# A two-layer encoder trunk: one-hot addition of the last two expert units, earlier gate weights, an earlier embedding product and x scaled ahead of its transposition

## Chip, cores and metric

The kernel runs on one core of one Trainium2 chip. The metric is device time in microseconds, lower is better: 1538.12 us, the median of three runs (1536.56 to 1542.2).

## What is computed

Two layers over 512 tokens of width 1024, all in float32. Each layer has attention in two branches, then a mixture of 32 experts, then a gated embedding. The part around the change, cut from the reference:

```python
x = x + hierarchical_moe(rmsnorm(x, g_ffn[i]), ...)   # top-1 of 4 groups, then top-2 of 8 experts
# per expert: hid = silu(xb @ w_gate[e]) * (xb @ w_up[e]); y = hid @ w_down[e]
# out[token] += gate * y, two experts per token
ple_gate = jax.nn.sigmoid(rmsnorm(x, g_ple[i]) @ w_ple_gate[i])
x = x + (p[i] @ w_ple[i]) * ple_gate
```

## The kernel before

The rows of x (512 x 1024) lie in on-chip memory as four tiles of 128 tokens. All other large buffers are slots of 8 KB per partition in one arena, numbered 0 to 18 (and 20); in odd layers slots 0 to 3 and 15 to 18 change places (`place`). PSUM has two banks for `proj`, two for `av` and four for `z`, each handed out in turn in the order of the program. The order of the instructions on an engine is set ahead of time by a scheduler that goes by the program's order and by estimated times; `tc.issue_after` puts one instruction behind another by hand. Each engine and each queue then works in that order.

**Experts.** The 32 experts are taken in pairs, with room for 64 tokens each, so that a unit is 128 rows on both halves of the array; a 17th unit in the middle takes tokens of an expert with more. The loop over units is at L1221. A unit goes through `fetch` (POOL gathers its rows), `turn` (transpositions, L1143), `up` (32 first-stage products, L1160, then the activation, `act`) and, one iteration later, `finish`: `down` (transposition L1172, copy `hid` L1174, 16 second-stage products L1179), two copies out of PSUM and a scatter by POOL's indirect DMA into `ybuf` in HBM (L1192). Weights come in loads of 1 MB on the SP queue (L1015), as far ahead as slots are free; `expert_slots` lays down which.

**Embedding.** Six units ahead of the end the loop loads the embedding rows (`praw`, L1226) and `w_ple`; `ple_rows` transposes and splits them five units ahead of the end (L1205), and `ple_product(t)` multiplies one tile of 128 tokens (12 products, L116 to L118) in each of the next four iterations, between a `down` and the next `up`.

**float32 products in three.** `split` makes two parts of a value: ACT copies it, rounded, to `hi` (L139, L142), VectorE forms the rest, `lo` (L140, L143). `mm` does hi x hi, lo x hi and hi x lo. Each gate weight is 8 such pieces (`Stream.split`); `gcol` is the norm's gain.

**The end of the experts.** All units but the last are scattered. When they are in `ybuf`, SP loads it back, both results of each token side by side (`yg`, L1257, four loads of 1 MB), with the first loads of the gate weights (L329) between them. `stored(t)` adds both to x with the token's gates `gm2` (L1267). The last unit isn't scattered: its result is split into `y`, a matrix `which` with a one where row and token meet is built, and a product with it (L1282) brings the rows to their tokens; L1285 adds them with the gates `gl`. `after` computes `gm2` and `gl` behind the routing. Then come, for each tile, the sum of squares (L1287), the reciprocal root `r` (L1289, L1290) and `turn_in`, which transposes x, unscaled, and splits it into `gT` (L289, L139, L140).

**The gate.** Two halves of two weights each; in each, four tiles by two weights (`PAIRED`), 24 products of 256 columns apiece. For each result the sigmoid is made of Abs, Exp, Ln and Exp on ACT with `r` as the scale of Abs (L1335), and on VectorE `pz = min(p r, 0)` (L1339) and a subtraction (L1340); then come the product with the embedding (L1343) and the addition to x (L1344). The third and fourth gate weight reuse the buffers of the first two for their `hi` part, so they are split behind the first half's products. In layer 0 POOL loads the next layer's first weight meanwhile (L1298).

Of the kernel before, what the change touches and what calls it, by code (L numbers as in the profile page):

```python
# [23 lines left out]
D = 1024  # L24
# [37 lines left out]
def trunk(ctx: ExitStack, tc: tile.TileContext, a, out):  # L62
# [240 lines left out]
    def turn_in(xs, hT, t):  # L303
        for h, p in transposed(xs):
            split(p, hT.t[h][:, :, t * 128:(t + 1) * 128])

    class Stream:
# [3 lines left out]
        def __init__(self, srcs, raws, his=(7, 8), pieces=1, first=(), eng=nc.vector, pool=(), depth=None, quick=()):  # L311
# [7 lines left out]
            self.nsplit = 0  # L319

# [53 lines left out]

        def get(self, ahead=1):
# [20 lines left out]
    for l in range(L):  # L396
# [3 lines left out]
        ws2 = Stream([(a["wple"][l], (128, 2, D))] + [(a["wpg"][l, c], std, gcol[:, 1]) for c in range(4)], (10, 6, 4, 9), his=(7, 8), pieces=8, first=(5,))  # L400
# [647 lines left out]
        def after():  # L1048
# [5 lines left out]
            gl2 = keep.tile([128, 2, NT], F32, name="gl2")  # L1054
            nc.vector.tensor_tensor(gl2, fo[:, :, :, NP - 1], fo[:, :, :, NE - 1], op=OP.add)
            nc.vector.scalar_tensor_tensor(gl2, rt, float(CAP), gl2, op0=OP.is_lt, op1=OP.mult)
            nc.vector.tensor_tensor(gl2, gl2, gm2, op=OP.mult)
            nc.vector.tensor_tensor(gm2, gm2, gl2, op=OP.subtract)
            nc.vector.tensor_tensor(gl, gl2[:, 0], gl2[:, 1], op=OP.add)
# [14 lines left out]
        gl = keep.tile([128, NT], F32, name="gl")  # L1074
# [91 lines left out]
        def down(u, sg):  # L1166
# [7 lines left out]
            nc.scalar.activation(hid, pt[:, :2 * n].rearrange("p (c n) -> p c n", c=2), AF.Copy)  # L1174
# [23 lines left out]
        halves, whole = [None], [None]  # L1198
# [10 lines left out]
        def ple_product(t):  # L1209

            wp = ws2.done[0]
            if t % 2 == 0:
                pp[t // 2] = slot(11 + t // 2, [128, 2, D], F32, f"pp{t // 2}")
            for h in range(2):
                p = p_proj()
                with tc.issue_after(halves[0]):
                    whole[0] = mm(p, lambda k: pT[:, k, t * 128:(t + 1) * 128], lambda k: wp[:, k, h * 512:(h + 1) * 512], 2).ins
                nc.scalar.activation(pp[t // 2][:, t % 2, h * 512:(h + 1) * 512], p, AF.Copy)

        last = None  # L1220
        for i, u in enumerate(units):  # L1221
            if i + 2 < len(units):
                gs.append(fetch(units[i + 2]))
            if i == len(units) - 6:
# [5 lines left out]
            if i == len(units) - 5:  # L1230
                ple_rows()
            if i == len(units) - 1:
                finish(*last)
# [202 lines left out]
```

## Time and profile before

| | |
|---|---|
| median of the runs | 1538.12 us (1536.56 to 1542.2) |
| profiled execution | 1539.81 us, its span 1538.1 us |
| mean granted TensorE clock | 0.976 |
| TensorE busy | 1453.9 us (95%) |
| VectorE busy | 714.8 us (46%) |
| ACT busy | 669.5 us (44%) |
| POOL busy | 114.8 us (7%) |
| DMA | 325.42 MB, mean 212 GB/s |

Times in the profile count from the first instruction. PE is TensorE, DVE is VectorE, ACT is ScalarE, SP and POOL issue DMAs; a q behind a name is that engine's instruction queue. A timeline's line gives start, length, engine, line of the kernel, operation, output<-input with shapes and count, and in brackets the idle time before it and what ended it. Matmuls overlap, so their single lengths are longer than their distance. Granted clock 1.00 is 2.4 GHz, 0.50 is 1.2 GHz.

### The profile page before, as it was taken

The numbers are of one execution on the slowest core, as the hardware profiler recorded it, in microseconds if no ns is written. First come the engines' busy times: TensorE is split into PE (matmuls) and PEld (weight loads), VectorE is DVE, ScalarE is ACT, GpSimd is POOL, SyncE is SP. The second block draws the span as 40 slices with busy tenths as digits, with TensorE's granted clock in tenths as the row PEclk, the third lists the DMA queues.
The fourth block names the chain that finished last, engine by engine and source line by source line (L and its number), as shares of the span: only waits on it lengthen the run. The fifth ranks groups of instructions, "written<-read, shape, count | busy, mean of one in ns | idle before, by whom it ended". The sixth has DMA issues, their size and how long they took to land. (4 is left out here: it accounts for less than half of the span.)

```text
span 1538.1 us, 21263 instructions
## 1 busy us (share of the span) xinstructions
PE 1453.9 (95%) x8212; PEld 1007.8 (66%) x8212; DVE 714.8 (46%) x1606; ACT 669.5 (44%) x1448; POOL 114.8 (7%) x113
## 2 busy tenths in 40 slices
PE   8999999999989998888999999999999999979886
PEld 7767886888963333336897688778898533334386
DVE  5574675544452121218836746654535321122186
ACT  5674455543322222325836745655532222222166
POOL 0000000000111111010210000000002111110002
PEclk9999999999989999998999999999999999999998
DMA  7210224325389999985121111252363899999731
GB/s 299 96 46 13 107 83 157 112 89 219 138 302 416 418 412 414 422 343 215 71 108 55 56 55 59 81 197 83 102 274 113 350 419 420 377 418 422 315 134 55
DMA packets 60780, 325.42 MB, mean 212 GB/s; under 512 B 11429, under 2 KB 11685, under 8 KB 28033
## 3 DMA queue, kind: packets, MB, share of 16 engines
q1 hardware_dynamic: 50272, 302.10, 49.8%
q0 software_dynamic: 9248, 17.70, 3.1%
q10 hardware_dynamic: 1152, 4.19, 0.7%
q8 instruction: 67, 1.10, 0.3%
q14 instruction: 41, 0.33, 0.1%
HBM read 312.04 MB, written 28.84 MB: 222 GB/s over the span
## 5 line engine op out<-in xcount | busy, mean ns | idle before, releaser
L1160 PE MATMUL proj<-raw,gT 128*64 128x512 f32 x1056 | 261.5, 600 | 4.1 <-issue 3.0
L140 DVE TENSOR_TENSOR wlo<-raw,whi 128x1024 fp32r<-128x1024 f32 (+1 forms) x108 | 121.4, 1141 | 125.4 <-ACT whi L139 123.9
L1160 PEld LDWEIGHTS proj<-raw,gT 128*64 128x64 f32 x1056 | 81.8, 137 | 146.1 <-issue 143.5
L1179 PE MATMUL z<-raw,hid 128*64 128x512 f32 x528 | 155.6, 636 | 2.0 <-ACT hid L1174 1.9
L139 ACT ACTIVATE whi<-raw 128x1024 fp32r<-128x1024 f32 (+1 forms) x108 | 104.8, 990 | 77.1 <-PE proj L117 45.6
L811 POOL TENSOR_TENSOR xs<-x,gb 128x512 f32<-128x512 f32 (+2 forms) x34 | 45.6, 1343 | 974.1 <-DVE x L855 809.2
L147 ACT ACTIVATE sgm<-proj 128x256 f32<-128x256 f32 (+1 forms) x34 | 13.0, 384 | 208.5 <-PE proj L1160 208.5
L117 PE MATMUL proj<-wlo,gTh 128*128 128x256 f32 x336 | 98.0, 292 | 4.6 <-DVE wlo L143 4.6
L1179 PEld LDWEIGHTS z<-raw,hid 128*64 128x64 f32 x528 | 45.2, 144 | 82.5 <-issue 73.0
L116 PE MATMUL proj<-whi,gTh 128*128 128x256 f32 x336 | 97.5, 290 | 1.4 <-ACT gTh L139 1.4
L118 PE MATMUL proj<-whi,gTl 128*128 128x256 f32 x336 | 97.5, 290 | 0.0
L1147 DVE COPY gT<-av 128x512 f32<-128x512 f32 (+1 forms) x32 | 21.5, 671 | 149.7 <-PE proj L1160 113.8
L118 PE MATMUL proj<-gTh,wlo 128*128 128x512 f32 x192 | 75.6, 394 | 0.0
L118 PE MATMUL proj<-hTh,wlo 128*128 128x512 f32 x192 | 75.6, 394 | 0.0
L117 PE MATMUL proj<-hTl,whi 128*128 128x512 f32 x192 | 75.6, 394 | 0.0
L117 PE MATMUL proj<-gTl,whi 128*128 128x512 f32 x192 | 75.6, 394 | 0.0
L116 PE MATMUL proj<-hTh,whi 128*128 128x512 f32 x192 | 75.5, 393 | 0.0
L116 PE MATMUL proj<-gTh,whi 128*128 128x512 f32 x192 | 75.5, 393 | 0.0
L116 PE MATMUL proj<-whi,mh 128*128 128x256 f32 x256 | 74.0, 289 | 0.0
L117 PE MATMUL proj<-wlo,mh 128*128 128x256 f32 x256 | 72.9, 285 | 0.0
L118 PE MATMUL proj<-whi,ml 128*128 128x256 f32 x256 | 72.6, 284 | 0.0
L117 PEld LDWEIGHTS proj<-wlo,gTh 128*128 128x128 f32 x336 | 65.9, 196 | 6.1 <-DVE wlo L143 6.0
(341 smaller groups left out, 3299.2 us busy)
## 6 DMA issues: line engine op xcount, KB each, us to landing
raw<-in_wgu_dram SPq DMA_DIRECT2D x132, 1024.0 KB
raw<-in_wdn_dram SPq DMA_DIRECT2D x66, 1024.0 KB
raw<-in_win_dram SPq DMA_DIRECT2D x37, 1024.0 KB
raw<-in_wo_dram SPq DMA_DIRECT2D x8, 1024.0 KB
yg<-ybuf SPq DMA_DIRECT2D x8, 1024.0 KB
raw<-in_wpg_dram SPq DMA_DIRECT2D x8, 1024.0 KB
ybuf<-zero SPq DMA_DIRECT2D x8, 512.0 KB
brw<-in_bra_dram SPq DMA_DIRECT2D x16, 256.0 KB
```

The lines of the kernel that those rows point to most:

```text
L116: nc.tensor.matmul(o, lhs.hi, rhs.hi, start=start, stop=False, **kw)
L117: nc.tensor.matmul(o, lhs.hi, rhs.lo, start=False, stop=False, **kw)
L118: return nc.tensor.matmul(o, lhs.lo, rhs.hi, start=False, stop=stop, **kw)
L139: r = nc.scalar.activation(dst.hi, src, AF.Copy)
L140: split_lo[0] = eng.tensor_tensor(dst.lo, src, f(dst.hi), op=OP.subtract)
L147: nc.scalar.activation(dst, src, AF.Abs)
L811: nc.gpsimd.tensor_tensor(xs[t][:, cs], x[:, t][:, cs], gb[:, cs], op=OP.mult)
L1147: nc.vector.tensor_copy(gT[h], src)
L1160: nc.tensor.matmul(p[r:r + CAP], gT[h][:, k, r:r + CAP], w[:, k], start=h + k == 0, stop=h + k == 4, tile_position=(0, r), skip_group_chec ...
L1179: halves[0] = nc.tensor.matmul(py[r:r + CAP], hid[:, c, r:r + CAP], w[:, c, h * 512:(h + 1) * 512], start=c == 0, stop=c == 1, tile_positi ...
```

## The change

- `praw` and `w_ple` are loaded 8 units ahead of the end, transposed 7 ahead; the eight half-tile products are done in six iterations: two, two, one, one, one, one.
- The last two units aren't scattered: unit 15's result is split into `y0` (slot 3) ahead of the last unit, the last one's into `y1`. `which`, `gl` and the one-hot products exist twice. `yg` lies in slots 0, 1, 2, 5.
- SP issues gate weight 1 ahead of `yg` 0, then weight 2, `yg` 1, weight 3, `yg` 2, `yg` 3; weight 4 goes into `yg` 1's slot, loaded behind tile 1. Weight 1's first four pieces are split behind unit 15's split and ahead of `y1`'s; weight 3 has `hi` in slot 9 and is split behind the last tile's transposition.
- x of each tile is scaled by `r` on ACT into `yg`'s second half, and this is transposed; the gate uses `sigmoid` without a scale.

```diff
         for h, p in transposed(xs):
-            split(p, hT.t[h][:, :, t * 128:(t + 1) * 128])
+            r = split(p, hT.t[h][:, :, t * 128:(t + 1) * 128])
+        return r, split_lo[0]
     class Stream:
...
                 self.done[i] = w
+        def begin(self, i):
+            self.load(i)
+            self.nsplit += 1
+            shape = list(self.srcs[i][1])
+            self.done[i] = Pair(slot(self.his[(self.nsplit - 1) % len(self.his)], shape, F32R, "whi"), self.low[i])
+        def piece(self, i, c):
+            w, c = self.done[i], slice(c, c + 1)
+            hi = split(self.raw[i][:, c], w[:, c], self.srcs[i][2][:, c])
+            self.apart(hi, self.pieced.setdefault(i, []), split_lo[0])
+            return hi, split_lo[0]
         def get(self, ahead=1):
...
         ws1 = streams[l]
-        ws2 = Stream([(a["wple"][l], (128, 2, D))] + [(a["wpg"][l, c], std, gcol[:, 1]) for c in range(4)], (10, 6, 4, 9), his=(7, 8), pieces=8, first=(5,))
+        ws2 = Stream([(a["wple"][l], (128, 2, D))] + [(a["wpg"][l, c], std, gcol[:, 1]) for c in range(4)], (10, 6, 4, 10, 1), his=(7, 8, 7, 9, 8), pieces=8, first=(5,))
         if l == 0:
...
             nc.vector.tensor_tensor(gm2, gate, bad, op=OP.mult)
-            gl2 = keep.tile([128, 2, NT], F32, name="gl2")
-            nc.vector.tensor_tensor(gl2, fo[:, :, :, NP - 1], fo[:, :, :, NE - 1], op=OP.add)
-            nc.vector.scalar_tensor_tensor(gl2, rt, float(CAP), gl2, op0=OP.is_lt, op1=OP.mult)
-            nc.vector.tensor_tensor(gl2, gl2, gm2, op=OP.mult)
-            nc.vector.tensor_tensor(gm2, gm2, gl2, op=OP.subtract)
-            nc.vector.tensor_tensor(gl, gl2[:, 0], gl2[:, 1], op=OP.add)
+            for j in range(2):
+                u = NP - 2 + j
+                gl2 = keep.tile([128, 2, NT], F32, name="gl2")
+                nc.vector.tensor_tensor(gl2, fo[:, :, :, u], fo[:, :, :, NP + u], op=OP.add)
+                nc.vector.scalar_tensor_tensor(gl2, rt, float(CAP), gl2, op0=OP.is_lt, op1=OP.mult)
+                nc.vector.tensor_tensor(gl2, gl2, gm2, op=OP.mult)
+                nc.vector.tensor_tensor(gm2, gm2, gl2, op=OP.subtract)
+                nc.vector.tensor_tensor(gl[:, j], gl2[:, 0], gl2[:, 1], op=OP.add)
             nc.vector.scalar_tensor_tensor(sp, rt, -float(CAP - 1), sp, op0=OP.add, op1=OP.mult)
...
             ws2.get(0)
-        def ple_product(t):
+        def ple_product(t, h):
             wp = ws2.done[0]
-            if t % 2 == 0:
+            if t % 2 == 0 and not h:
                 pp[t // 2] = slot(11 + t // 2, [128, 2, D], F32, f"pp{t // 2}")
-            for h in range(2):
-                p = p_proj()
-                with tc.issue_after(halves[0]):
-                    whole[0] = mm(p, lambda k: pT[:, k, t * 128:(t + 1) * 128], lambda k: wp[:, k, h * 512:(h + 1) * 512], 2).ins
-                nc.scalar.activation(pp[t // 2][:, t % 2, h * 512:(h + 1) * 512], p, AF.Copy)
+            p = p_proj()
+            with tc.issue_after(halves[0]):
+                whole[0] = mm(p, lambda k: pT[:, k, t * 128:(t + 1) * 128], lambda k: wp[:, k, h * 512:(h + 1) * 512], 2).ins
+            nc.scalar.activation(pp[t // 2][:, t % 2, h * 512:(h + 1) * 512], p, AF.Copy)
         last = None
...
                 gs.append(fetch(units[i + 2]))
-            if i == len(units) - 6:
+            if i == len(units) - 8:
                 praw = slot(12, [128, NT, 256], F32, "praw")
...
                 ws2.load(0)
-            if i == len(units) - 5:
+            if i == len(units) - 7:
                 ple_rows()
             if i == len(units) - 1:
-                finish(*last)
                 break
...
             last, curT = (u, sg), nxtT
-            if i >= len(units) - 5:
-                ple_product(i - len(units) + 5)
-        which = wk.tile([128, 512], F32R, name="which", tag="gT", bufs=4)
+            if i >= len(units) - 7:
+                for k in ((0, 1), (2, 3), (4,), (5,), (6,), (7,))[i - len(units) + 7]:
+                    ple_product(k // 2, k % 2)
         tokens = wk.tile([128, 512], F32, name="tokens", tag="gT", bufs=4)
         nc.gpsimd.iota(tokens, pattern=[[1, 512]], base=0, channel_multiplier=0, allow_small_or_imprecise_dtypes=True)
-        token = wk.tile([128, 1], F32, name="token")
-        nc.vector.tensor_copy(token, idx[:, u:u + 1])
-        nc.vector.tensor_scalar(which, tokens, token, None, op0=OP.is_equal)
-        ygs = []
-        for t in range(NT):
-            ygs.append(slot(t, [128, 2, D], F32, "yg"))
-            nc.sync.dma_start(ygs[t], ybuf.rearrange("(i t p) d -> t p i d", i=2, p=128)[t])
-            if t < 2:
-                ws2.load(t + 1)
-        ws2.split(1)
-        sg = up(u, curT)
-        ws2.split(2)
-        def stored(t):
-            for i in range(2):
-                nc.vector.scalar_tensor_tensor(x[:, t], ygs[t][:, i], gm2[:, i, t:t + 1], x[:, t], op0=OP.mult, op1=OP.add)
-        gT = Halves([15, 16, 17, 18], "gT")
-        stored(0)
-        y = slot(20, [128, 2, D], F32R, "y")
-        for h, py in enumerate(down(u, sg)):
-            split(py, Pair(y[:, 0, h * 512:(h + 1) * 512], y[:, 1, h * 512:(h + 1) * 512]))
-        ws2.load(3)
-        ws2.load(4)
-        for t in range(NT):
-            if t:
-                stored(t)
+        which = []
+        def find(u):
+            which.append(wk.tile([128, 512], F32R, name="which", tag="gT", bufs=4))
+            token = wk.tile([128, 1], F32, name="token", tag="token", bufs=2)
+            nc.vector.tensor_copy(token, idx[:, u:u + 1])
+            nc.vector.tensor_scalar(which[-1], tokens, token, None, op0=OP.is_equal)
+        ys = [slot(3, [128, 2, D], F32R, "y0"), None]
+        def halved(j, py, h):
+            y = ys[j]
+            return split(py, Pair(y[:, 0, h * 512:(h + 1) * 512], y[:, 1, h * 512:(h + 1) * 512]))
+        def added(j, t):
             for h in range(2):
...
                 for c in range(2):
-                    nc.tensor.matmul(p, which[:, t * 128:(t + 1) * 128], y[:, c, h * 512:(h + 1) * 512],
+                    nc.tensor.matmul(p, which[j][:, t * 128:(t + 1) * 128], ys[j][:, c, h * 512:(h + 1) * 512],
                                      start=c == 0, stop=c == 1)
                 xc = x[:, t][:, h * 512:(h + 1) * 512]
-                nc.vector.scalar_tensor_tensor(xc, p, gl[:, t:t + 1], xc, op0=OP.mult, op1=OP.add)
+                nc.vector.scalar_tensor_tensor(xc, p, gl[:, j, t:t + 1], xc, op0=OP.mult, op1=OP.add)
+        find(last[0])
+        for h, py in enumerate(down(*last)):
+            halved(0, py, h)
+        before = hidden[0], split_lo[0]
+        ygs = []
+        for t in range(NT):
+            if t < 3:
+                ws2.load(t + 1)
+            ygs.append(slot((0, 1, 2, 5)[t], [128, 2, D], F32, "yg"))
+            nc.sync.dma_start(ygs[t], ybuf.rearrange("(i t p) d -> t p i d", i=2, p=128)[t])
+        sg = up(u, curT)
+        find(u)
+        def stored(t):
+            for i in range(2):
+                nc.vector.scalar_tensor_tensor(x[:, t], ygs[t][:, i], gm2[:, i, t:t + 1], x[:, t], op0=OP.mult, op1=OP.add)
+        gT = Halves([15, 16, 17, 18], "gT")
+        ws2.begin(1)
+        with tc.issue_after(before[0].ins), tc.issue_after(before[1].ins):
+            parts = [ws2.piece(1, c) for c in range(4)][-1]
+        stored(0)
+        added(0, 0)
+        stored(1)
+        added(0, 1)
+        ys[1] = slot(20, [128, 2, D], F32R, "y1")
+        for h, py in enumerate(down(u, sg)):
+            with tc.issue_after(parts[0].ins), tc.issue_after(parts[1].ins):
+                results = halved(1, py, h)
+        for c in range(4, KT):
+            ws2.piece(1, c)
+        ws2.split(2)
+        for t in range(NT):
+            if t > 1:
+                stored(t)
+                added(0, t)
+            added(1, t)
             ss = npool.tile([128, 1], F32, name="ss", tag="ss", bufs=4)
...
             nc.scalar.activation(r, r, AF.Exp, scale=-0.5)
-            turn_in(x[:, t], gT, t)
+            for h in range(2):
+                nc.scalar.activation(ygs[t][:, 1, h * 512:(h + 1) * 512], x[:, t][:, h * 512:(h + 1) * 512], AF.Copy,
+                                     scale=r)
+            last_turn = turn_in(ygs[t][:, 1], gT, t)
+            if t == 1:
+                ws2.load(4)
+        with tc.issue_after(last_turn[0].ins), tc.issue_after(last_turn[1].ins):
+            ws2.split(3)
         work2.close()
...
                 p = banks[t] if wide else banks[t][:, cc * 256:(cc + 1) * 256]
-                r = rs[:, t:t + 1]
                 with tc.high_priority() if not wide else ExitStack():
-                    s = wk.tile([128, 512], F32, name="ps", tag="ps", bufs=3)[:, :n]
-                    nc.scalar.activation(s, p, AF.Abs, scale=r)
-                    nc.scalar.activation(s, s, AF.Exp, scale=-1.0)
-                    nc.scalar.activation(s, s, AF.Ln, bias=1.0)
-                    z = wk.tile([128, 512], F32, name="pz", tag="pz", bufs=3)[:, :n]
-                    nc.vector.tensor_scalar(z, p, r, 0.0, op0=OP.mult, op1=OP.min)
-                    nc.vector.tensor_tensor(s, z, s, op=OP.subtract)
-                    nc.scalar.activation(s, s, AF.Exp)
+                    s = wk.tile([128, 512], F32, name="ps", tag="ps", bufs=4)[:, :n]
+                    sigmoid(s, p)
                     cs = slice(c0 * 256, c0 * 256 + n)
```

## Rows read from the trace of the kernel before

**Rows 1.** Timeline of TensorE at the embedding's transpositions, both layers

```profile
619.56 1.97 PE L1205 MATMUL z<-ident,praw 128*128 128x128 f32 x8 [5.09 <-DMA praw<-in_p_dram]
...
1380.18 1.97 PE L1205 MATMUL z<-ident,praw 128*128 128x128 f32 x8 [4.76 <-DMA praw<-in_p_dram]
...
1383.05 4.78 PE L1179 MATMUL z<-raw,hid 128*64 128x512 f32 x16 [0.47 <-ACT hid L1174]
```

**Rows 2.** Timeline of the SP queue, layer 1: start, us, line, what is issued

```profile
1323.20 4.45 SPq L1015 DMA_DIRECT2D raw<-in_wdn_dram  x2
...
1359.02 0.33 SPq L1226 DMA_DIRECT2D praw<-in_p_dram  x1
...
1450.61 0.38 SPq L1257 DMA_DIRECT2D yg<-ybuf  x1
```

**Rows 3.** Busy time by stretch, layer 1: us, each engine's busy us, granted clock, DMA share, GB/s

```profile
1335.00:1340.00 5.00, 5.00 (x24) 1.70 (x22) 1.01 (x2) 0.38 (x1) 1.96 (x2) 1.00 0.97 346
...
1380.00:1385.00 5.00, 4.35 (x16) 2.66 (x18) 2.73 (x5) 3.81 (x7) 0.00 (x0) 0.50 1.02 423
...
1435.00:1440.00 5.00, 5.00 (x20) 2.59 (x15) 0.69 (x1) 1.20 (x2) 0.99 (x1) 1.00 0.89 374
...
1440.00:1445.00 5.00, 5.00 (x25) 2.23 (x26) 0.69 (x1) 1.19 (x2) 0.00 (x0) 1.00 0.47 189
...
1450.00:1455.00 5.00, 1.31 (x6) 0.29 (x2) 1.27 (x3) 2.01 (x5) 0.00 (x0) 0.86 0.69 247
...
1465.00:1470.00 5.00, 2.33 (x11) 1.81 (x11) 5.00 (x11) 2.14 (x5) 0.00 (x0) 0.73 1.04 424
```

**Rows 4.** Timeline of TensorE from the last product to the gate, layer 1

```profile
1437.08 0.51 PE L116 MATMUL proj<-whi,pT 128*128 128x512 f32 x1
...
1440.08 3.70 PE L1179 MATMUL z<-raw,hid 128*64 128x512 f32 x16
...
1443.57 7.09 PE L1160 MATMUL proj<-raw,gT 128*64 128x512 f32 x32
...
1453.93 0.66 PE L1172 MATMUL z<-ident,sgm 128*128 128x128 f32 x2 [3.28 <-DVE sgm L1081]
...
1455.06 6.31 PE L1179 MATMUL z<-raw,hid 128*64 128x512 f32 x16 [0.47 <-ACT hid L1174]
...
1466.19 0.39 PE L116 MATMUL proj<-whi,gTh 128*128 128x256 f32 x1 [0.69 <-ACT gTh L139]
...
1471.29 0.41 PE L118 MATMUL proj<-whi,gTl 128*128 128x256 f32 x1
...
1482.65 1.18 PE L1282 MATMUL z<-y,which 128*128 128x512 f32 x4
```

**Rows 5.** Busy time by stretch where the second pair of gate weights is split

```profile
740.00:745.00 5.00, 2.72 (x13) 2.32 (x14) 4.97 (x10) 3.75 (x10) 2.01 (x3) 0.87 0.57 210
...
1500.00:1526.00 26.00, 24.14 (x194) 23.33 (x192) 21.24 (x38) 20.34 (x46) 5.97 (x4) 1.00 0.11 41
```

**Rows 6.** POOL's scatter of a unit's results, layer 1, and how long scatters take to land

```profile
1438.63 0.99 POOL L1192 DMA_INDIRECT ybuf<-ring,dst  x1 [11.54 <-DVE ring L1189]
...
DMA to landing us min/median/max: 8.5/8.5/8.6
```

**Rows 7.** Groups by shape between 1440 and 1500 us: count, busy us, mean ns

```profile
L1267 DVE SCALAR_TENSOR_TENSOR x<-yg,gm,x 128x1024 f32<-128x1024 f32 x8 | 10.1, 1276 | 0.0
...
L1285 DVE SCALAR_TENSOR_TENSOR x<-z,gl,x 128x512 f32<-128x512 f32 x8 | 5.8, 745 | 0.2
...
L1287 ACT ACTIVATE yg<-x 128x1024 f32<-128x1024 f32 x4 | 4.2, 1055 | 2.5 <-DVE x L1285 2.5
...
L139 ACT ACTIVATE gTh<-z 128x512 fp32r<-128x512 f32 x8 | 4.7, 594 | 8.8 <-PE z L289 8.8
...
L140 DVE TENSOR_TENSOR gTl<-z,gTh 128x512 fp32r<-128x512 f32 x8 | 5.5, 690 | 1.8 <-ACT gTh L139 1.6
...
L1339 DVE TENSOR_SCALAR pz<-proj,rs 128x512 f32<-128x512 f32 x2 | 1.5, 748 | 0.2 <-ACT ps L1335 0.2
```

More of the change, by code (lines that the diff above doesn't have):

```diff
@@ L319, in __init__ @@
             self.nsplit = 0
+            self.pieced = {}
         def load(self, i, eng=nc.sync, parts=1):
@@ L1073, in trunk @@
         gm2 = wt("gm2", [128, 2, NT])
-        gl = keep.tile([128, NT], F32, name="gl")
+        gl = keep.tile([128, 2, NT], F32, name="gl")
         routing.close()
@@ L1173, in down @@
             hid = wk.tile([128, 2, 128], F32, name="hid", tag="hid", bufs=2)[:, :, :n]
-            nc.scalar.activation(hid, pt[:, :2 * n].rearrange("p (c n) -> p c n", c=2), AF.Copy)
+            hidden[0] = nc.scalar.activation(hid, pt[:, :2 * n].rearrange("p (c n) -> p c n", c=2), AF.Copy)
             for h in range(2):
@@ L1196, in trunk @@
         pp = [None, None]
-        halves, whole = [None], [None]
+        halves, whole, hidden = [None], [None], [None]
         def ple_rows():
@@ new lines, in halved @@
+        def halved(j, py, h):
[3 more added lines that the diff above has]
+            for h in range(2):
+                p = p_z()
+                for c in range(2):
+                    nc.tensor.matmul(p, which[j][:, t * 128:(t + 1) * 128], ys[j][:, c, h * 512:(h + 1) * 512],
+                                     start=c == 0, stop=c == 1)
+                xc = x[:, t][:, h * 512:(h + 1) * 512]
+                nc.vector.scalar_tensor_tensor(xc, p, gl[:, j, t:t + 1], xc, op0=OP.mult, op1=OP.add)
@@ L1269, in trunk @@
         gT = Halves([15, 16, 17, 18], "gT")
+        ws2.begin(1)
+        with tc.issue_after(before[0].ins), tc.issue_after(before[1].ins):
+            parts = [ws2.piece(1, c) for c in range(4)][-1]
         stored(0)
-        y = slot(20, [128, 2, D], F32R, "y")
+        added(0, 0)
+        stored(1)
+        added(0, 1)
+        ys[1] = slot(20, [128, 2, D], F32R, "y1")
         for h, py in enumerate(down(u, sg)):
-            split(py, Pair(y[:, 0, h * 512:(h + 1) * 512], y[:, 1, h * 512:(h + 1) * 512]))
-        ws2.load(3)
-        ws2.load(4)
+            with tc.issue_after(parts[0].ins), tc.issue_after(parts[1].ins):
[3 more added lines that the diff above has]
+        ws2.split(2)
         for t in range(NT):
-            if t:
+            if t > 1:
                 stored(t)
-            for h in range(2):
-                p = p_z()
-                for c in range(2):
-                    nc.tensor.matmul(p, which[:, t * 128:(t + 1) * 128], y[:, c, h * 512:(h + 1) * 512],
-                                     start=c == 0, stop=c == 1)
-                xc = x[:, t][:, h * 512:(h + 1) * 512]
-                nc.vector.scalar_tensor_tensor(xc, p, gl[:, t:t + 1], xc, op0=OP.mult, op1=OP.add)
+                added(0, t)
+            added(1, t)
             ss = npool.tile([128, 1], F32, name="ss", tag="ss", bufs=4)
@@ L1290, in trunk @@
             nc.scalar.activation(r, r, AF.Exp, scale=-0.5)
-            turn_in(x[:, t], gT, t)
+            for h in range(2):
+                nc.scalar.activation(ygs[t][:, 1, h * 512:(h + 1) * 512], x[:, t][:, h * 512:(h + 1) * 512], AF.Copy,
[5 more added lines that the diff above has]
+            ws2.split(3)
         work2.close()
```

## Prediction

> **What bounds the kernel now.** I read the busy shares first, then TensorE's timeline through the last expert units, then the busy time by stretch, and last the queues that feed them (SP and POOL). TensorE is busy for 95% of the span, so time can come only from places where it waits or runs at its lower clock. The end of each layer has three. Numbers are of layer 1 unless said otherwise; layer 0 shows the same sequence some 760.6 us earlier (the same transposition at 619.56 and at 1380.18 [rows 1]).
>
> First, the embedding's rows: TensorE stands for 5.09 us (layer 0) and 4.76 us until `praw` lands [rows 1]. The reader is to see that SP issues it at 1359.02 [rows 2], 21.2 us before the first transposition, behind a full queue (share 1.02), and that the granted clock afterwards is 0.50 (1.2 GHz) [rows 3]: the 16 second-stage products of a unit take 4.78 us there [rows 1] and 3.70 at the full clock [rows 4].
>
> Second, the passage from the last unit to the gate: that unit's first stage starts at 1443.57 and takes 7.09, its activation leaves TensorE idle for 3.28, the second stage runs at the low clock (6.31), and the gate's first product at 1466.19 has its third only at 1471.29 [rows 4]. From 1465 on VectorE is busy for 5.00 of 5 us and TensorE for 2.33 [rows 3]. What ends this passage is a chain: the scatter of unit 15, `yg` issued behind it at 1450.61 [rows 2], sums on VectorE, transpositions.
>
> Third, the passage between the two pairs of gate weights: TensorE has 2.72 of 5 us in layer 0, and 24.14 of 26 in layer 1 [rows 5].
>
> **Embedding earlier.** Today TensorE wants `praw` 16.4 us after its issue and gets it after 21.2. Two units earlier the issue follows the load at 1323.20 [rows 2], where fewer bytes move (346 GB/s, later 423) [rows 3] and less is queued. I take the wait as gone, with its 4.76 us and the clock's 1.08: the last unit starts 5.8 us earlier, near 1437.8. Lower bound 0 (the wait moves along). The eight products only change place. Before unit 14's results are scattered 3.5 tiles' worth of them stand in place of 3; a tile takes 3.0 us (1437.08 to 1440.08) [rows 4]. That scatter thus starts 5.8 - 1.5 = 4.3 us before 1438.63 [rows 6], at 1434.3.
>
> At 1335 the DMA share is 0.97 at 346 GB/s [rows 3]. The Trainium skill, DMA: Bandwidth & Descriptors, section Issuing engines are not separate DMA queues, says that all DMAs run on the same 16 engines and interleave; so 1.5 MB moved into that stretch displaces other loads as long as the share is near 1. Read by bytes, it would fit there, and the stream of expert weights would end 3.6 us earlier (1.5 MB at 423 GB/s): some 1519 us in all. The trace's share agrees with the rule, and the sum takes nothing.
>
> **Unit 15 stays on chip.** Its copies become a split of about the same cost, and its scatter goes. `yg` waits for unit 14's scatter, which lands 8.5 us after its start [rows 6], at 1442.8. SP's order is then the first gate weight (issued before), `yg` 0, weight 2, `yg` 1, weight 3, `yg` 2, `yg` 3; all behind `yg` 0 wait with it. A megabyte at 420 GB/s takes 2.5 us; the 247 GB/s of the 5 us from 1450 mean that the flow began 1.5 us after the issue at 1450.61 [rows 2, 3]. With 0.4 for SP's issue, `yg` 0 is there at 1447.2, `yg` 1 at 1452.2.
>
> **What is late next.** The last unit's three z buffers are allocated behind four of the one-hot products of tiles 0 and 1, and there are four buffers. Its second half so waits until VectorE has added tile 1: `yg` 1, two sums of 1.28, one addition of 0.75 [rows 7], 1455.5. Its eight products take half of 6.31 at the low clock [rows 4]: 1458.7. Then come split (0.59 and 0.69), one-hot product (0.5), addition (0.75), Square (1.06) and, new on the path, the scaled copy (0.6, as the ACT copy of its size), transposition (0.66) and two half splits (1.9) [rows 4, 7]; with 0.9, chosen, for two one-column steps and handovers the gate runs from 1466.3 in place of 1471.3: **5.0 us per layer**. The scaled copies are 8 x 0.6 us of ACT per layer; beyond the first tile they lie beside TensorE's products. The first weight's split moves into time in which VectorE and ACT are idle, beside the last unit's first stage; without that cover it stands in front of the first tile, as now.
>
> **More products.** Sixteen more one-hot products per layer; four take 1.02 us (1482.65 to 1483.67, by the start of the next work) [rows 4]. Those of tiles 0 and 1 fall into TensorE's idle time, those of tiles 2 and 3 among the gate's products, where it is full: **2.0 us per layer** more. VectorE, after the last unit, has 4 sums, 12 additions and 8 half splits, 5.1 + 9.0 + 5.5 = 19.6 us, against 10.2 + 6.0 + 5.5 = 21.7 now [rows 7], so it does not become the bound.
>
> **Third gate weight in buffers of its own**, loaded and split during the first pair's products. Today's waits there go: 26 - 24.14 = 1.9 us in layer 1, and 5 - 2.72 = 2.3 in layer 0, with the clock's 0.87 and its tail 3.0 [rows 5]. Bounds: 0, if the fourth weight is late in its place, and these values, since nothing more is lost there. I take **1.9 and 3.0**.
>
> **x scaled beforehand.** Nine `pz` operations per layer go, 0.75 each for the wide ones [rows 7]. They ran beside ACT's chain; I take 0.5 us at the very end of layer 1, bounds 0 and 6.7 per layer. Five more small operations behind the routing lie under the first unit's products; uncovered they cost under 3.7 us (five of 0.745, the nearest row) [rows 7]. In layer 0 POOL's load of the next layer's first weight now waits for the last `yg` buffer; it is wanted only in the gate's second half.
>
> **Sum:** 2 x (-5.0 + 2.0) - 1.9 - 3.0 - 0.5 = -11.4 us. The profiled execution took 1539.81 (span 1538.1), 1.7 above the median of 1538.12: 1528.4 on its own time, **1526.7** on the median's.
>
> **Rivals.** *More comes back* (0.15). The scatter lands sooner, or the stream of weights ends earlier; `yg` and the gate move with it, one for one. With 5 us for the scatter and 1.5 us from the stream both layers gain 5 us more: 1517. For it: the stream thins from 1440 (share 0.47). Against it: the scatter starts while the share is still 0.89 or more [rows 3].
>
> *Nothing is left* (0.24). The wait for `praw` reappears two units earlier. Then unit 14's scatter starts 1.5 us later than today, `yg` 1 lands at 1458, and the gate starts at 1472: 0.7 + 2.0 lost per layer, 1.9, 3.0 and 0.5 back, 1538. The same comes out if split and additions, in VectorE's order, hold the first tile by 5 us. For it: the share near 1 at the new place.
>
> *Slower: the sums stand in front of the last unit's activation* (0.11). VectorE works in order. If the sums of tiles 0 and 1 are placed ahead of that unit's three activation steps, these wait for `yg` 1, two sums and two additions, to 1456.3. Some 2 us of activation, 1.1 of transposition and copy, the second stage at 6.31 and the chain above put the gate at 1474, and with a scatter no earlier than today's at 1481. Per layer that is 2.7 to 10 and 2.0 lost: 1542 to 1557, say 1548. It decides from a gate start of 1472 on. For it: an order set by estimated landing times can be wrong. Against it: by the program's order the activation comes first, and the four buffers hold the second stage in any case.
>
> **Chances.** The forecast has 0.50, its own range 1519 to 1534. Half a per cent, 7.7 us, is about what a measurement of this kernel can tell from no change: faster is below 1530.4. That takes four fifths of the forecast, all of the first rival and little of the second: 0.56. Within 0.5%: the rest of the forecast and most of the second rival, 0.33; slower 0.11. The range 1513 to 1541 takes in the first two rivals and leaves out the slower one's body.
>
> **What would show it.** Right: no wait of TensorE on `praw`; `yg` issued some 8 us earlier; the last unit's second half held until VectorE has added tile 1; the gate's third product 28.5 us or less after the last unit's start; no wait on `wlo` at the second pair. Wrong: a wait on `praw` two units earlier, VectorE standing on `yg` ahead of the last activation, or a gate start after 1472.

## The result: slower, and the profile after

The changed kernel takes 1567.6 us (median of four runs, 1565.73 to 1568.37) against 1538.69 for the kernel before: a ratio of 1.0179, 95% interval 1.0166 to 1.0193. The profiled execution took 1567.79, its span 1566.1. Predicted were 1526.7 us, 1513 to 1541.

TensorE is busy for 1472.8 us in place of 1453.9, so the loss is not idle time alone. In layer 1, against the kernel before, the bulk of the last unit's first stage starts 23.9 us later (1467.47 for 1443.57 [rows 4]; two of its products stand at 1465.58, among one-hot products) and the gate's first product comes 34.7 us later. These figures hold the loss of layer 0 too, where the same happens.

**Ahead of the last unit.** Nothing waits for `praw` any more (a wait of 1.21 us for the split of `pT` is new). The first row below is TensorE's timeline at its transposition (L1223, once L1207); in [rows 1] it stood for 4.76 us. The other rows show what came in its place.

```profile
1359.26 1.04 PE L1223 MATMUL z<-ident,praw 128*128 128x128 f32 x8
...
1383.18 0.41 PE L1190 MATMUL z<-ident,sgm 128*128 128x128 f32 x2 [1.83 <-DVE sgm L1099]
1383.52 5.34 PE L1197 MATMUL z<-raw,hid 128*64 128x512 f32 x12
1391.80 4.50 PE L1178 MATMUL proj<-raw,gT 128*64 128x512 f32 x18
...
1403.75 0.41 PE L1190 MATMUL z<-ident,sgm 128*128 128x128 f32 x2 [1.83 <-DVE sgm L1099]
```

L1190 is the transposition of a unit's activation (L1172 before), L1197 the second stage (L1179 before). The reader is to see two things. The transposition of unit k stands inside the second stage of unit k-1, right behind unit k's first stage, so TensorE waits for the activation each time: 1.83, 1.83, 1.83, 1.61 and 1.58 us in the last five units of this kind. And the 16 second-stage products come as 4 and 12. The kernel before has this form too, but only in its last two iterations with embedding products; the other two run clean (timeline of the kernel before):

```profile
1398.70 3.65 PE L1179 MATMUL z<-raw,hid 128*64 128x512 f32 x16
...
1413.22 1.93 PE L1179 MATMUL z<-raw,hid 128*64 128x512 f32 x4
1415.88 0.41 PE L1172 MATMUL z<-ident,sgm 128*128 128x128 f32 x2 [0.73 <-DVE sgm L1081]
1416.21 3.65 PE L1179 MATMUL z<-raw,hid 128*64 128x512 f32 x12
```

Twelve take as long as sixteen, and the four cost 1.93 us extra. The products of the two experts of a unit lie on the two halves of the array. Taken one by one in the trace, the sixteen start in pairs, a pair every 0.43 us; the four start singly, 0.43 us apart, and of the twelve four pairs and then four single ones. The trace names no half; that the four are of one expert alone is inferred from this spacing. In two of the five places the twelve behind the wait take 5.34 us (in the others 3.65), since the granted clock is lower there: 0.69 and 0.66 over 5 us, between its levels of 1.2 GHz (0.50) and 2.4. The view is the busy time by stretch of the changed kernel; its last three numbers are granted clock, DMA share and GB/s:

```profile
1385.00:1390.00 5.00, 5.00 (x13) 1.95 (x10) 0.69 (x1) 0.60 (x1) 0.00 (x0) 0.69 1.03 421
1405.00:1410.00 5.00, 5.00 (x13) 1.66 (x11) 0.53 (x1) 0.60 (x1) 0.00 (x0) 0.66 1.01 423
```

**From the last unit to the gate** (TensorE's timeline of the changed kernel):

```profile
1467.47 7.08 PE L1178 MATMUL proj<-raw,gT 128*64 128x512 f32 x30
1484.09 0.69 PE L1190 MATMUL z<-ident,sgm 128*128 128x128 f32 x2 [9.53 <-DVE x L1289]
1485.25 6.24 PE L1197 MATMUL z<-raw,hid 128*64 128x512 f32 x16 [0.47 <-ACT hid L1192]
...
1497.52 1.97 PE L289 MATMUL z<-ident,yg 128*128 128x128 f32 x8 [4.10 <-ACT yg L1336]
1499.14 1.90 PE L1286 MATMUL z<-y,which 128*128 128x512 f32 x4
...
1500.88 0.28 PE L116 MATMUL proj<-whi,gTh 128*128 128x256 f32 x1
```

The last transposition waits 9.53 us for an addition to x, where it waited 3.28 for the activation [rows 4]; the first transposition of x waits for the scaled copies (L1336). VectorE's own timeline shows what it did in that time:

```profile
1471.16 0.49 DVE L1274 TENSOR_SCALAR which<-tokens,token 128x512 fp32r<-128x512 f32 x1 [5.86 <-PE proj L1178]
...
1477.61 2.85 DVE L143 SCALAR_TENSOR_TENSOR wlo<-raw,gcol,whi 128x256 fp32r<-128x256 f32 x7
1480.38 1.28 DVE L1307 SCALAR_TENSOR_TENSOR x<-yg,gm,x 128x1024 f32<-128x1024 f32 x1
1481.58 0.48 DVE L143 SCALAR_TENSOR_TENSOR wlo<-raw,gcol,whi 128x256 fp32r<-128x256 f32 x1
1481.97 1.28 DVE L1307 SCALAR_TENSOR_TENSOR x<-yg,gm,x 128x1024 f32<-128x1024 f32 x1
1483.28 1.41 DVE L1289 SCALAR_TENSOR_TENSOR x<-z,gl,x 128x512 f32<-128x512 f32 x2
...
1490.21 1.40 DVE L1289 SCALAR_TENSOR_TENSOR x<-z,gl,x 128x512 f32<-128x512 f32 x2
```

Seven pieces of weight 1, then tile 0's sums with an eighth piece between them, then tile 0's additions, which give z buffers back. The first of them releases the transposition; the activation had been ready since 1477.7, so the hold is 6.4 of the 9.53 us. Tile 1's additions come only at 1490.21, when the second stage (from 1485.25 on, without a break) is nearly through. None of these rows waits for `yg`, which had landed at 1468.27 for tile 0 and at 1473.32 for tile 1. From the activation to the gate VectorE has hardly a pause: 22.77 us of 23.59 here, 11.87 of 18.40 in the same passage of the kernel before (busy time by stretch, kernel before first; the third busy time is VectorE's):

```profile
1453.80:1472.20 18.40, 13.32 (x41) 6.53 (x42) 11.87 (x20) 8.89 (x21) 0.00 (x0) 0.69 1.02 419
1477.61:1501.20 23.59, 12.27 (x37) 5.97 (x38) 22.77 (x36) 11.30 (x25) 0.00 (x0) 0.65 0.16 65
```

ACT then shows what stands between the additions and the first transposition:

```profile
1495.00 1.06 ACT L1331 ACTIVATE yg<-x 128x1024 f32<-128x1024 f32 x1 [2.87 <-DVE x L1289]
...
1496.75 1.33 ACT L1336 ACTIVATE yg<-x,rs 128x512 f32<-128x512 f32 x2
```

### The profile page after: what moved, and what is told of

The parts are those of the page before. It is cut to its first block, busy times and chain, and to the rows that moved or that the text cites. A ratio compares the mean times of both kernels' runs of the same rounds, so it can differ in the third digit from the quotient of the medians.

```text
span 1566.1 us, 21371 instructions
## 1 busy us (share of the span) xinstructions
PE 1472.8 (94%) x8244; PEld 1009.2 (64%) x8244; DVE 712.0 (45%) x1620; ACT 678.8 (43%) x1466; POOL 112.3 (7%) x111
## 5 line engine op out<-in xcount | busy, mean ns | idle before, releaser
L1197 PE MATMUL z<-raw,hid 128*64 128x512 f32 x528 | 165.9, 644 | 1.9 <-ACT hid L1192 1.9
L1197 PEld LDWEIGHTS z<-raw,hid 128*64 128x64 f32 x528 | 48.1, 144 | 87.3 <-issue 78.1
L116 PE MATMUL proj<-whi,gTh 128*128 128x256 f32 x336 | 96.3, 287 | 0.7 <-ACT tm L577 0.7
L116 PE MATMUL proj<-gTh,whi 128*128 128x512 f32 x192 | 75.5, 393 | 0.0
L116 PE MATMUL proj<-hTh,whi 128*128 128x512 f32 x192 | 75.5, 393 | 0.0
L116 PE MATMUL proj<-whi,mh 128*128 128x256 f32 x256 | 74.0, 290 | 0.0
```

Of the source, the lines that this page charges most:

```text
L116: nc.tensor.matmul(o, lhs.hi, rhs.hi, start=start, stop=False, **kw)
L1197: halves[0] = nc.tensor.matmul(py[r:r + CAP], hid[:, c, r:r + CAP], w[:, c, h * 512:(h + 1) * 512], start=c == 0, stop=c == 1, tile_positi ...
```

## Experiments

All times are medians; each run was compared with the kernel before on its own chip (1539.4 to 1540.9 us there). "Ties" are `tc.issue_after` edges on TensorE:

```diff
 # down(): the next unit's transposition, and each second-stage product
+with tc.issue_after(halves[0]):
     nc.tensor.transpose(pt[:, c * n:(c + 1) * n], ...)
...
+with tc.issue_after(halves[0]):
     halves[0] = nc.tensor.matmul(py[r:r + CAP], ...).ins
```

**The embedding's move alone.**

```diff
 # kernel before
-if i == len(units) - 6:
+if i == len(units) - 8:
-if i == len(units) - 5:
+if i == len(units) - 7:
...
+for k in ((0, 1), (2, 3), (4,), (5,), (6,), (7,))[i - len(units) + 7]:
+    ple_product(k // 2, k % 2)
```

> The kernel before with only the embedding moved: its loads 8 units ahead of the end, its transpositions 7 ahead, its products in six iterations as in the change; everything from the last unit on as before. Theory A (the order of the second-stage products and transpositions that the scheduler writes once the embedding stands two units earlier costs some 10 us per layer, as units 10 to 15 show between the two traces): 1539 + 20 = about 1559 us, 1553 to 1563, no wait on praw, waits of 1.5 to 1.9 us for the activation in the last units. Rival B (the move gives back its 4.8 + 1.1 us per layer as predicted, and the loss lies in the end of the experts): about 1527 us.

1550.1 us, ratio 1.0059 (1.0042 to 1.0076): 10 us slower with nothing else changed. The waits of 1.58 to 1.83 us are there in five places, as in the changed kernel, and `praw` is not waited for. That is theory A at half its size; rival B falls. TensorE's waits for the activation in layer 1's expert units (us in total, times, longest; kernel before, then this run):

```profile
PE z L1172 <- DVE sgm L1081: 5.8, 4, 1.7
PE z L1172 <- DVE sgm L1081: 10.4, 6, 1.8
```

**The embedding put back into the changed kernel** (the same edit backwards).

> The changed kernel with the embedding back in its old place (loads 6 units ahead of the end, transpositions 5 ahead, four whole tiles). Theory A: units 10 to 15 run as before, with the wait on praw of 4.8 to 5.1 us back; 9 to 11 us per layer come back: 1545 to 1550 us. Rival B (the embedding's move is a gain of 5.8 us per layer that the end hides): 1576 to 1580 us.

1554.2 us: 13.4 less than the changed kernel. Rival B falls again. A's 1545 to 1550 was too low: the form of the kernel before comes back with its own two broken units and with a wait for `praw` (2.6 and 4.3 us).

**Ties on the changed kernel.**

> The changed kernel with the second-stage products of a unit tied to their program order, and the next unit's transposition tied behind them. Theory A: the broken pairs (1.7 us per unit), the waits for the activation (1.6 to 1.8) and the low clock behind them go in the units with embedding products, 8 to 10 us per layer: 1547 to 1552 us. Rival B (the loss lies in the end of the experts alone): 1564 to 1568 us.

1543.4 us, ratio 1.0022 (1.0012 to 1.0031): 24.2 us back, more than A expected. All waits for the activation ahead of the last unit are gone and the second stage is whole:

```profile
1402.30 0.66 PE L1161 MATMUL av<-ident,gb 128*128 128x128 f32 x4 [0.78 <-DVE gT L1165]
1402.88 3.65 PE L1199 MATMUL z<-raw,hid 128*64 128x512 f32 x14
...
1459.41 0.69 PE L1191 MATMUL z<-ident,sgm 128*128 128x128 f32 x2 [9.56 <-DVE x L1291]
```

Its end is still that of the changed kernel: 9.56 us of hold.

**Ties on the kernel before, and with the embedding moved.**

> The kernel before with the same ties on the second-stage products and transpositions, nothing else. Theory A says that the kernel before, too, pays for the broken form in its last two units before the last (waits of 0.73 and 1.58 us, unpaired products 1.7 us each time): 2 to 4 us per layer, 1532 to 1536 us. Rival: there the form costs nothing, 1539 to 1541 us.

> The kernel before with the ties and the embedding moved as in the change. If the prediction's term for the move was right and only the order spoiled it (theory A), the 4.8 to 5.1 us of the wait for praw and 1.1 of the clock come back in each layer against the run with the ties alone: 10 to 12 us less than that, 1521 to 1527 us. Rival G (the moved loads displace the weights of the experts, so TensorE waits for those in place of praw): the same time as the run with the ties alone.

1530.8 (ratio 0.9936, 0.9918 to 0.9954) and 1529.1 us (0.9931, 0.9912 to 0.995). The ties alone are worth 10 us: more than expected, and more than any part of the change. The move on top of them gives 1.7 by the medians, not 10 to 12, and the intervals overlap, so even the 1.7 isn't clear of noise; yet the wait for `praw` (6.44 us in the run with ties alone) is gone. No wait on weights took its place, so rival G's reason isn't what the trace shows either. The experts' stretch of layer 1, from the first expert product to the end of unit 15's second stage, tells more (kernel before; changed; ties; ties and move; changed with ties; columns as above, after PE, PEld, DVE, ACT and POOL):

```profile
1207.18:1443.57 236.39, 222.21 (x977) 85.61 (x979) 45.86 (x91) 56.34 (x126) 30.67 (x31) 0.97 0.99 402
```
```profile
1222.05:1463.87 241.82, 228.00 (x977) 85.21 (x977) 45.62 (x93) 56.22 (x126) 30.65 (x31) 0.98 0.98 398
```
```profile
1204.84:1436.81 231.97, 218.31 (x977) 82.60 (x979) 45.88 (x91) 56.12 (x126) 30.67 (x31) 0.97 0.99 406
```
```profile
1200.92:1431.46 230.54, 222.60 (x977) 82.55 (x978) 45.49 (x91) 55.63 (x126) 30.58 (x31) 0.99 0.99 409
```
```profile
1212.14:1439.50 227.36, 219.42 (x977) 81.92 (x977) 46.15 (x93) 55.68 (x126) 30.67 (x31) 1.00 1.01 413
```

From the third row to the fourth the move takes 5.7 us of idle time from TensorE (231.97 - 218.31 = 13.66 to 230.54 - 222.60 = 7.94), about what the prediction had. But TensorE's busy time grows by 4.3 us, with the same 977 products and no lower clock. Of the 746 records of products on half the array, 72 start alone in the trace (no other within 0.15 us) with the move, 56 without; in the kernel before and in the move without ties it is 68 and 92. So the order still seems to cost much of what the wait gave back; these ties don't hold the first-stage products. The clock isn't the cause of the loss either: its mean is 0.97 in the kernel before and 0.98 in the changed one.

Length times rate is 94 to 96 MB in each. The DMA engines are full throughout, and 424 GB/s is the most that any 20 us reached, so some 222 us (94 MB) is the least for this stretch, an estimate from these rows. With ties TensorE is busy for 94 to 97% of it as well. That the stream of weights limits the move's gain isn't shown: with ties and move TensorE waits for no weights here.

**Wider ties** (the first stage's products too, and the transposition behind the next unit's first stage).

```diff
 # up()
+behind = whole[0] if h + k + r == 0 and whole[0] else ups[0]
+with tc.issue_after(behind):
+    ups[0] = nc.tensor.matmul(p[r:r + CAP], ...).ins
```

> The kernel before with the embedding moved and with wider ties: the first-stage products too are tied to their program order, and a unit's transposition stands behind the next unit's first stage. Theory A, extended (with the narrow ties the iterations with embedding products still take 18.3, 16.9 and 16.5 us where the kernel before needs 14.5, since first-stage products of one side stand alone): 2 to 4 us in each of three units, 8 us per layer, 1513 to 1519 us. Rival H (the DMA share is 1.0 from 1230 to 1420 in every run so far, so the stream of weights is the next bound): waits on raw take the place of what is saved, 1526 to 1530 us.

1530.1 us, nothing gained. H's time, but not by its reason: no wait on weights; nine waits for `hid`, 4.4 us in all, took the place of the breaks. A's extension compared unequal work: the kernel before does some of the later units' transpositions earlier, so its 14.5 us hold less.

**x unscaled** (ties kept).

```diff
-for h in range(2):
-    nc.scalar.activation(ygs[t][:, 1, h * 512:(h + 1) * 512], ..., AF.Copy, scale=r)
-last_turn = turn_in(ygs[t][:, 1], gT, t)
+last_turn = turn_in(x[:, t], gT, t)
 # and the gate's sigmoid as in the kernel before
```

> The changed kernel with the ties, and with x transposed unscaled and the factor in the gate's sigmoid, as in the kernel before. Theory E (the sum of squares, the root and the two scaled copies now stand in front of the first transposition: 3.7 us from 1469.43 to 1473.10 in the tied run): the gate starts 3 to 4 us earlier per layer, less up to 1 us for the longer sigmoid: 1535 to 1540 us against 1543 tied. Rival: the copies lie beside VectorE's sums and weight pieces, and the time stays at 1542 to 1545 us.

1535.7 us, 7.7 less (9.2 by the ratios to the kernel before, as the two runs are from different chips): theory E. From the end of unit 15's second stage to the gate's third L116 product it is 32.7 us in place of 37.2 in layer 1, 32.5 in place of 36.8 in layer 0. TensorE at the first transposition of x, scaled and unscaled:

```profile
1471.95 1.97 PE L289 MATMUL z<-ident,yg 128*128 128x128 f32 x8 [4.11 <-ACT yg L1338]
```
```profile
1467.77 1.31 PE L289 MATMUL z<-ident,x 128*128 128x128 f32 x8 [0.95 <-DVE x L1291]
```

**The gate weights of the change in the kernel before** (ties, embedding moved; then with the wider ties).

```diff
-(10, 6, 4, 9), his=(7, 8), pieces=8, first=(5,))
+(10, 6, 4, 10, 1), his=(7, 8, 7, 9, 8), pieces=8, first=(5,))
...
+if t == 1:
+    ws2.load(4)
...
+with tc.issue_after(last_turn[0].ins), tc.issue_after(last_turn[1].ins):
+    ws2.split(3)
```

> The kernel before with the narrow ties and the embedding moved, and with the third and fourth gate weight loaded and split as in the change. The prediction's term: 1.9 + 3.0 us less than without it: 1523 to 1526 us. Rival: the splits only move and the second half's start is set by something else, 1527 to 1531 us.

> The kernel before with the wider ties, the embedding moved and the gate weights of the change; the last two units' sums as in the kernel before. By theory A, extended, and the prediction's term for the weights: 1508 to 1515 us. By rival H and without the term: 1526 to 1530 us.

1522.2 us (0.988, 0.9864 to 0.9897), 6.9 less than without (on another chip), and 1524.8, which is 5.3 less than the 1530.1 with wider ties alone (on the same chip). The prediction's term of 4.9 holds and is a little small; the wider ties give nothing here either. The mechanism is the predicted one: TensorE's waits for weight pieces in layer 0's gate shrink (without, then with; narrow ties), and in layer 1's, 1.9 us before, they are gone.

```profile
PE proj L117 <- DVE wlo L143: 2.7, 3, 1.1
PE proj L117 <- DVE wlo L143: 0.4, 1, 0.4
```

**Three tries on the end of the changed kernel.** First, the last unit's second stage ahead of the sums and additions, without ties; second, with ties, all pieces of weight 1 ahead of the last activation, weight 2's behind tile 1; third, with ties and x unscaled, the second stage first and weight 2's pieces behind tile 0.

```diff
 # all three (the second keeps stored(0), tied behind the activation)
-stored(0)
-added(0, 0)
-stored(1)
-added(0, 1)
 ys[1] = slot(20, [128, 2, D], F32R, "y1")
 for h, py in enumerate(down(u, sg)):
...
 # the second
+with tc.issue_after(parts[0].ins), tc.issue_after(parts[1].ins):
+    sg = up(u, curT)
```

> The changed kernel with the last unit's second stage and its split ahead, in the program, of the sums and additions of tiles 0 and 1, so that its z buffers wait for no addition; the experts' part as it is. Theory C (the wait of 9.5 us in front of that unit's transposition is a hold of z buffers, and its end is on the path): the transposition follows the activation within 1 us, and the gate starts 4 to 7 us earlier per layer: 1553 to 1560 us. Rival D (the hold is beside the path: yg and VectorE's sums set the gate's start in any case): 1565 to 1569 us.

> The changed kernel with the ties and another order at the end of the experts: weight 1's eight pieces stand ahead of the last unit's activation, tile 0's two sums right behind it, the last unit's second stage ahead of all one-hot products (so its z buffers wait for no addition), and weight 2's eight pieces behind tile 1. Theory F (VectorE's order sets the gate's start): tile 0's additions end 7 to 9 us earlier than in the tied run, so does the gate's first product; 14 to 18 us over both layers, 1525 to 1530 us. Rival D (the landing of yg sets it): tile 0's sums start no earlier than 1455 in layer 1 and the gate at most 3 us earlier, 1537 to 1543 us.

> The changed kernel with the narrow ties, x unscaled, the last unit's second stage ahead of all one-hot products, and weight 2's pieces tied behind tile 0's transposition. Theory F (z buffers held by additions, and weight pieces ahead of tile 0's sums on VectorE, set the gate's start): no wait of TensorE for x in front of the last transposition, gate 4 to 7 us earlier per layer than without it, 1522 to 1528 us. Rival D (weight 1 and yg land too late in any order): 1533 to 1537 us.

1568.3 us (1557.72 to 1573.9, a spread that stays unexplained), 1556.9 and 1538.1: theories C and F missed all three. D comes near the first and the third in time, but no row there waits for `yg`. In the first the hold is gone (3.28 us again), but on VectorE weight 2's eight pieces now stand ahead of tile 0's additions, and the gate starts no earlier:

```profile
1486.05 2.60 DVE L1307 SCALAR_TENSOR_TENSOR x<-yg,gm,x 128x1024 f32<-128x1024 f32 x2
1488.57 3.25 DVE L143 SCALAR_TENSOR_TENSOR wlo<-raw,gcol,whi 128x256 fp32r<-128x256 f32 x8
1491.73 2.72 DVE L1289 SCALAR_TENSOR_TENSOR x<-z,gl,x 128x512 f32<-128x512 f32 x4
```

In the second, the tie put ACT's pieces, and with them a wait for weight 1, ahead of the last activation (ACT's timeline):

```profile
1458.37 3.30 ACT L142 ACTIVATE whi<-raw,gcol 128x256 fp32r<-128x256 f32 x8 [12.05 <-DMA raw<-in_wpg_dram]
1461.58 0.36 ACT L147 ACTIVATE sgm<-proj 128x256 f32<-128x256 f32 x1
```

In the third, the passage is 29.5 us in layer 0 (32.5 with the hold) and 32.0 in layer 1 (32.7), and the gate gives back more than that, in part in three waits of TensorE for weight 2's pieces per layer (1.5 us), which the run with the hold doesn't have. The hold was real, but behind it stands VectorE's list of work.

**Unit 15 on chip or scattered, in one order.** Both runs have ties, the moved embedding, the gate weights of the change and x unscaled; weight 1's pieces stand between the last activation and its split, weight 2's behind tile 0.

```diff
 for h, py in enumerate(down(u, sg)):
+    if not h:
+        ws2.begin(1)
+        with tc.issue_after(acted[0].ins), tc.issue_after(hidden[0].ins):
+            parts = [ws2.piece(1, c) for c in range(KT)][-1]
+    with tc.issue_after(parts[0].ins), tc.issue_after(parts[1].ins):
+        if not h:
+            stored(0)
```

> The kernel before with the narrow ties, the embedding moved, the gate weights of the change (weight 1 issued ahead of the first yg), and weight 1's eight pieces tied between the last unit's activation and its split, weight 2's behind tile 0's transposition; unit 15 is scattered as before. Theory F (from the last activation on VectorE's list of work sets the gate's start; there 3.2 us of pieces stood between tile 0's additions): the third gate product comes 2 to 3 us earlier after the last unit's start (25 to 26 us in place of 27.3 to 28.6), 1514 to 1519 us. Rival D (the landing of yg behind unit 15's scatter sets it): a wait of VectorE on yg takes the place of the pieces, 1521 to 1526 us.

> The same order of pieces, sums and additions in the changed kernel with the narrow ties and x unscaled, so that it differs from the run above in unit 15 staying on chip. If the prediction's premise holds (yg behind unit 15's scatter is late, and without it the gate starts 5 us earlier per layer for 2 us of one-hot products), it is 4 to 6 us faster than that run. Theory F: yg is not waited for in either, and four more additions for tiles 0 and 1 (2.7 us) and sixteen more products cost 2 to 4 us per layer: 4 to 8 us slower than that run, 1519 to 1527 us.

Scattered: 1520.1 us, ratio 0.9868 (0.9833 to 0.9902), the fastest of all and 20 us below the kernel before. Theory F's passage came (25.8 us in layer 1 for 28.2), its time nearly (1514 to 1519 expected). On chip: 1529.9 us (0.9929, 0.9904 to 0.9954), 9.7 more. VectorE's timeline of the scattered run:

```profile
1440.31 3.28 DVE L143 SCALAR_TENSOR_TENSOR wlo<-raw,gcol,whi 128x256 fp32r<-128x256 f32 x8 [1.92 <-ACT whi L142]
1444.67 1.29 DVE L1285 SCALAR_TENSOR_TENSOR x<-yg,gm,x 128x1024 f32<-128x1024 f32 x1 [1.08 <-DMA yg<-ybuf]
```

Here `yg` is waited for: 1.08 us in layer 1, nothing in layer 0. That is about all that keeping unit 15 on chip could save in this passage, and the passage is indeed no shorter with it (25.3 and 26.6 us for 26.1 and 25.8, layers 0 and 1). The price is paid in the gate: from its third L116 to its last product layer 1 takes 55.3 us for 51.2. Of the 4.1, the one-hot products that stand there account for 2.4 (18 records for 8) and waits for 1.5. The waits of TensorE there (us in total, times, longest) have this row on chip and none scattered:

```profile
PE proj L117 <- DVE wlo L143: 1.5, 3, 0.8
```

## Why the prediction was wrong

The runs form a ladder from the kernel before to the changed one: before 1540; ties 1530.8; embedding moved 1529.1; gate weights 1522.2; order of the pieces (and weight 1 issued ahead of `yg`) 1520.1; unit 15 on chip 1529.9; the change's order at the end 1535.7; x scaled 1543.4; no ties 1567.6. The medians are from different chips, on which the kernel before differs by 1.5 us, so single steps are no better than that: the move behind the ties (1.7) and the order of the pieces (2.1) are not clear of noise.

- **Embedding earlier.** The step that failed is "The eight products only change place". The wait for `praw` went, as said, but the order of TensorE's instructions, which the scheduler writes, changed with the move: the move alone lost 10 us where the last units were to start 11.6 earlier (5.8 per layer), and the ties took 24.2 off the changed kernel, though only 10 off the kernel before. That estimated arrivals made the scheduler split the pairs is argued from its design; that the order is the cause is shown. Even with the ties the move gave only 1.7 us, since TensorE's busy time grew by 4.3 of the 5.7 us of idle time that it took away in layer 1.
- **The rule on the DMA engines.** DMA share and rate agree with what the prediction cited from the Trainium skill (DMA: Bandwidth & Descriptors, section Issuing engines are not separate DMA queues): 94 to 96 MB at 398 to 413 GB/s in every version. The prediction rightly took nothing for an earlier end of the stream.
- **Unit 15.** "What ends this passage is a chain: the scatter of unit 15, `yg` issued behind it" was the wrong reading. In layer 1 of the kernel before no instruction of VectorE in this stretch waits on `yg`; in layer 0 one wait of 5.6 us is put down to it, but in front of the split of `y`, which doesn't read it and waits as long for ACT's copy in layer 1 (VectorE in layers 0 and 1 of the kernel before):

```profile
698.53 0.69 DVE L140 TENSOR_TENSOR y<-z,y 128x512 fp32r<-128x512 f32 x1 [5.63 <-DMA yg<-ybuf]
699.13 1.28 DVE L1267 SCALAR_TENSOR_TENSOR x<-yg,gm,x 128x1024 f32<-128x1024 f32 x1
...
1459.42 0.69 DVE L140 TENSOR_TENSOR y<-z,y 128x512 fp32r<-128x512 f32 x1 [5.63 <-ACT y L139]
1460.03 1.27 DVE L1267 SCALAR_TENSOR_TENSOR x<-yg,gm,x 128x1024 f32<-128x1024 f32 x1
```

  The 5.0 us per layer of the sum are in truth the embedding's 5.8 less 0.8: the predicted passage from the last unit's start to the gate's third product, 28.5 us, is longer than the 27.7 of [rows 4]. So the 5.0 fell with the embedding's term, and the passage itself took 35.5 us (1465.58 to 1501.11). Keeping unit 15 on chip cost 9.7 us over both layers in the direct comparison, of which the prediction had 4.0 as products.
- **The z buffers and VectorE's list.** That the last unit would be held for z buffers was right; but the hold stands in front of its transposition and ends with tile 0's first addition, not in front of its second half until tile 1 is added. That VectorE's order, not `yg`, could prolong it was right too; but the rival put the sums ahead of the activation, where the weight pieces stood ahead of the sums. The step that failed here is the count of VectorE's work after the last unit: 19.6 us, "so it does not become the bound". It has four sums, twelve additions and no weight pieces; in the trace all eight sums, all sixteen additions and the sixteen pieces of two weights stand behind the activation. The sum had the split of weight 1 in "time in which VectorE and ACT are idle"; it came behind the activation, though weight 1 had landed at 1460.47. In the program the pieces stand behind `up`, which holds the activation.
- **x scaled beforehand.** The copies' latency was in the chain (0.6 us and 0.9 for small steps), the direct comparison with an unscaled transposition was not: Square, two one-column steps and the first of two copies of 0.71 stand in front of the first transposition, 4.3 to 4.5 us per layer by the passage with and without them. Term: 0.5 gained; measured: 7.7 lost by the medians.
- **Third gate weight.** Right: 4.9 forecast, 6.9 and 5.3 measured.

The slower rival (0.11) named the right engine and the wrong place; its 1542 to 1557 are still short of 1567.6, since the prediction had no rival in which the embedding's move makes the expert units themselves slower.

## What to carry over

When a scheduler writes the order, moving a load moves more than the load: compare the instruction order on the bottleneck engine before costing a move at its wait, and tie what must stay together. Before removing something late, find an instruction that waits for it; a chain told from issue times is not a wait. Count all the work that an engine has in a passage, not only the part that changes, before saying that it doesn't become the bound. A step put in front of a transposition on the path costs its whole latency there, however short each instruction is.

## What the runs showed of the hardware

Two halves of the array: 16 products (128 rows, 64 columns) that start in pairs take 3.65 us, 12 of which four start singly also 3.65, and four that start singly 1.88 to 1.93. The Trainium skill, TensorEngine Tiling (Array Packing), section Tiling Modes, says that tiles run matmuls in parallel; the trace agrees, as long as the products start in pairs. Two products that start singly between products of the full array hold TensorE for 1.00 us (1400.12 to the next start at 1401.12 with ties and the move), where in a run of 32 (7.09 us) two take 0.44. DMA held 418 to 424 GB/s in stretches of 20 us and more.
